# Negated row maxima of two heads turned by one group of F32R passes a unit

## The chip, the cores and the metric

One core of a Trainium2 chip. The metric is device time in microseconds (us): the median of the runs of the kernel before is 2976.83 us (three runs, 2974.4 to 2983.3).

## What is computed

One layer of a hybrid encoder over 2048 tokens of width 1024: a joint input projection; attention with 8 query heads over 2 key heads of width 64, beside a state space mixer (SSM); an output projection; a feed-forward network; a final norm. The change lies in the attention:

```
s = einsum('bqgrd,bkgd->bgrqk', q_blk, k) * scale
p = softmax(s, axis=-1)
o = einsum('bgrqk,bkgd->bqgrd', p, v)
```

The softmax subtracts each row's maximum before the exponential. Here the maximum is taken of scores that are computed once for that purpose, and its negative is added to the scores inside the matmul that makes them again, as one more operand row.

## The kernel before

The attention is cut into 16 units of 512 queries by two heads. For each unit, `prep_q` (line 685) loads and transposes the queries; `prep_max` (line 707) computes the scores of 32 blocks (4 groups of 512 keys, 2 heads, 4 blocks of 128 queries) with queries on the partitions (line 718), and VectorE (DVE) reduces each to its row maxima (line 719). `unit` (line 766) then computes the scores again with keys on the partitions: two passes a tile of 128 keys by 512 queries, `ka` with `qa` (line 790) and `kb` with `qb` (line 791), the exponential on ScalarE (ACT, line 793), and the product with the values (line 776). The sums of the exponentials are kept on DVE and GpSimd (POOL, lines 781 and 784).

The upper 64 partitions of `kb` hold ones (line 666), those of `qb` hold, for each query, the negative maximum in one row and zeros in the others. Their product adds the negative maximum to each score. The maxima come out of the reduction with queries on the partitions, and have to be turned to lie along a row. For this `mn`, two buffers for alternate units, has a block of 64 columns for each of the 8 (head, query block) pairs, all zero but for column 0, into which line 725 writes. Line 729 multiplies each block, as the stationary operand, with the fp32 identity: 4 fp32 matmuls of 128 columns a head, into the upper 64 partitions of one PSUM bank `ps_mt`. Line 730 copies them into `qb` of that head (ACT). The bank is the only one of the pool `ps_m` (tag "am"); the transposed queries (`ps_qt`, line 693), the sums and the transposed outputs (`ps_rs`, `ps_rt`, `ps_ot`, lines 742 to 755) take it in turn.

F32R is the 4-byte type that a matmul takes in a single pass; a plain fp32 matmul shows as two records in the trace. The scores run in F32R: `qa`, `qb`, `ka`, `kb` are written in it.

What sets the order: while `unit` goes through its 16 key tiles, it takes steps of the preparation of later units (`advance`, line 814, four yields a key tile, up to two units ahead) and of the SSM (`bg_ssm`, line 917), until its eight chunks are used up around unit 9. The program runs under a planner (`schedule_with_timeline_sim`, line 1497) that lays out each engine's queue at build time from simulated times; on the chip each engine goes through its queue in that order. After the attention the output projection (line 996) and the feed-forward products (lines 1241 and 1371) have their PE order pinned.

Of the kernel before, what the change touches and what calls it, by code (L numbers as in the profile page):

```python
# [9 lines left out]
F32 = mybir.dt.float32  # L10
F32R = mybir.dt.float32r
AF = mybir.ActivationFunctionType
# [5 lines left out]
P = 128  # L18
# [3 lines left out]
HD = 64  # L22
# [46 lines left out]
def tile_encoder(ctx: ExitStack, tc: tile.TileContext, I, O, stop=None, dbg=None):  # L69
    nc = tc.nc  # L70
    V = nc.vector
    A = nc.scalar
    GP = nc.gpsimd
    T = nc.tensor
# [6 lines left out]
    def const(shape, name, dt=F32):  # L81
        return cp.tile(shape, dt, tag=name, name=name)
# [4 lines left out]
    ident = const([P, P], "ident")  # L87
# [48 lines left out]
    MUL, ADD, SUB = ALU.mult, ALU.add, ALU.subtract  # L136
# [499 lines left out]
    MUL, ADD, SUB = ALU.mult, ALU.add, ALU.subtract  # L636
    with ExitStack() as p2:
# [8 lines left out]
        kp = p2.enter_context(tc.tile_pool(name="kp", bufs=1, reuse_waits="tile"))  # L646
# [5 lines left out]
        def scores(u, name):  # L652
            return (next(turn) if u else ps_1).tile([P, 512], F32, tag="s1", name=name)

        def misc(name, tag="am"):
            return (ps_m if tag == "am" else ps_c).tile([P, 512], F32, tag=tag, name=name)

        lo, hi = slice(0, HD), slice(HD, P)
        ka = [[pool.tile([P, 512], F32R, tag=f"ka{i}{g}", name=f"ka{i}{g}") for g in range(4)] for i, pool in enumerate((eq, kp))]
        mn = [kp.tile([P, 8, HD], F32, tag=f"mn{i}", name=f"mn{i}") for i in range(2)]  # L660
        kb = [[kp.tile([P, 512], F32R, tag=f"kb{i}{g}", name=f"kb{i}{g}") for g in range(4)] for i in range(NKV)]
        for t in mn:
            GP.memset(t, 0.0)
        for i in range(NKV):
            for g in range(4):
                GP.memset(kb[i][g][hi].bitcast(F32), 1.0)
# [1 line left out]
        def prep_k(g, first):  # L668

            pt = scores(0, "ps_kt")  # L670
            for j in range(4):
                T.transpose(pt[:, P * j:P * (j + 1)], k_sb[g][:, j].rearrange("q h e -> q (h e)"), ident)
            for half in (lo, hi):
                if first:
                    A.copy(ka[0][g][half], pt[lo])
                else:
                    A.copy(ka[1][g][half], pt[hi])
            if not first:
                for i, own in enumerate((lo, hi)):
                    V.tensor_sub(kb[i][g][lo], pt[own], ka[i][g][own])  # L680
# [26 lines left out]
        def prep_max(u):  # L707

            kv = (u % 4) // 2
            qa, qb = units[u]  # L710
            mx = eq.tile([P, 8, 4], F32, tag="mx", name="mx", bufs=2)
            for f in range(4):
                if u == 0 and f == 3:
                    prep_k(3, True)
                for h in range(2):
                    for j in range(4):
                        p1_ = scores(u, "ps_s1")
                        T.matmul(p1_, qa[h][:, P * j:P * (j + 1)], ka[kv][f], start=True, stop=True)  # L718
                        red = V.reduce_max(mx[:, 4 * h + j, f:f + 1], p1_, axis=AX.X)  # L719
                        yield  # L720
            maxima.append(red)
            m8 = aq.tile([P, 8], F32, tag="m8", name="m8")
            V.reduce_max(m8, mx, axis=AX.X)
            mt = mn[u % 2]
            V.tensor_scalar(mt[:, :, 0], m8, -1.0, None, op0=MUL)
            for h in range(2):
                pm = misc("ps_mt")
                for j in range(4):
                    T.matmul(pm[hi, P * j:P * (j + 1)], mt[:, 4 * h + j, :], ident, start=True, stop=True)
                A.copy(qb[h][hi], pm[hi])  # L730
                yield

        def finish(u, po, acc):
# [70 lines left out]
        def prep_all():  # L804
            for u in range(1, 16):
                for g in (prep_q(u), prep_max(u)):
                    for _ in g:
                        yield u
            yield 16
# [111 lines left out]
        with tc.high_priority(KOFF):  # L921
            for g in range(3):
                prep_k(g, True)
            for _ in chain(prep_q(0), prep_max(0)):
                pass
            for g in range(4):
                prep_k(g, False)
# [573 lines left out]
```

## Time and profile before

| | |
|---|---|
| median of three runs | 2976.83 us |
| the profiled execution: time, span | 2980.86 us, 2979.1 us |
| mean granted clock of TensorE, share of full speed | 0.961 |
| busy time of PE, PE weight loads, DVE, ACT, POOL | 2795.3, 2039.3, 1964.0, 1255.7, 1326.3 us |
| attention units (first to last start of a pass of line 790) | 379.9 to 1338.6 us |

Times in the trace count from the start of the span. PE is TensorE's matmul side, PEld its weight loads, which overlap it. A PE record's duration is its latency; back to back, records overlap, so the distance of two starts is what a pass costs in the queue. A line of a timeline merges records of one kind that follow each other: its second number reaches from the first start to the last end. "Idle before" is the time in which the engine waited, with what ended it.

### The profile page before, as it was taken

Reading aid. Unit: us, or ns where it says so; the run is one execution under the profiler, and the core shown is the slowest. Engines: PE = TensorE matmul, PEld = TensorE weight load, DVE = VectorE, ACT = ScalarE, POOL = GpSimd, SP = SyncE. Lnnn points to the kernel's source line nnn. Section 1 sums busy time; section 2 is a strip of 40 time slices with the busy share of each in tenths; the row PEclk is TensorE's granted clock in tenths of the full one; section 3 lists DMA queues with packets and bytes.
Section 4 is the critical chain, followed back from the end, with each engine's and each line's share of the span. In section 5 each row is a group of like instructions: output and inputs, shape, how many; then the busy total and the mean of one; then the engine's idle time right before and its main releaser. Section 6 shows DMA issues by size and latency. Waiting matters only on the chain. (4 is left out here: it accounts for less than half of the span.)

```text
span 2979.1 us, 37166 instructions
## 1 busy us (share of the span) xinstructions
PE 2795.3 (94%) x13020; PEld 2039.3 (68%) x13020; DVE 1964.0 (66%) x2815; ACT 1255.7 (42%) x2609; POOL 1326.3 (45%) x1122
## 2 busy tenths in 40 slices
PE   6998988978988899998998999999999999999998
PEld 4776844544444455546886788887878888888876
DVE  6879977677877755655666777777244677775243
ACT  3654554544444455553334434445222344443222
POOL 3648467868888887542334333331001333321000
PEclk8999999989998999998999999999999999999999
DMA  7764221111110010003447333338664333336573
GB/s 214 219 231 144 98 72 43 50 46 46 47 50 25 29 36 11 8 11 124 142 134 243 118 113 114 113 111 297 206 233 152 117 114 114 113 108 235 191 235 118
DMA packets 306506, 359.42 MB, mean 121 GB/s; under 512 B 50104, under 2 KB 222864, under 8 KB 305296
## 3 DMA queue, kind: packets, MB, share of 16 engines
q1 hardware_dynamic: 306320, 357.06, 36.8%
q8 instruction: 102, 1.67, 0.2%
q14 instruction: 84, 0.69, 0.1%
HBM read 249.53 MB, written 107.45 MB: 120 GB/s over the span
## 5 line engine op out<-in xcount | busy, mean ns | idle before, releaser
L1241 PE MATMUL ps_ha<-xc,w 128*128 128x512 f32 x2112 | 499.4, 392 | 14.3 <-ACT w L1201 8.4
L1371 PE MATMUL ps_f<-wo,act_i 128*128 128x512 f32 x2112 | 485.2, 392 | 6.8 <-DVE x2r L1389 4.3
L1241 PEld LDWEIGHTS ps_ha<-xc,w 128*128 128x128 f32 x2112 | 399.3, 189 | 99.9 <-ACT w L1201 8.8
L1371 PEld LDWEIGHTS ps_f<-wo,act_i 128*128 128x128 f32 x2112 | 399.3, 189 | 92.0 <-DVE x2r L1389 6.1
L719 DVE TENSOR_REDUCE mx<-ps_s 128x1 f32<-128x512 f32 x512 | 333.4, 682 | 110.5 <-PE ps_s L718 108.5
L1267 POOL TENSOR_TENSOR act_o<-th,act_o 128x512 fp32r<-128x512 f32 x88 | 115.2, 1309 | 486.4 <-ACT act_o L1266 473.0
L1202 DVE TENSOR_TENSOR wo<-wo_raw,wo 128x512 fp32r<-128x512 f32 x176 | 121.4, 702 | 295.3 <-ACT wo L1201 295.3
L1202 DVE TENSOR_TENSOR w<-w_raw,w 128x512 fp32r<-128x512 f32 x220 | 207.1, 959 | 117.3 <-ACT w L1201 117.3
L718 PE MATMUL ps_s<-ka,qa 128*128 128x512 f32 x512 | 212.2, 454 | 47.1 <-DVE mx L719 45.4
L1241 PE MATMUL ps_hb<-xc,w 128*128 128x512 f32 x1056 | 247.3, 389 | 0.0
L374 PE MATMUL ps_z<-whi,ht 128*128 128x512 f32 (+1 forms) x768 | 226.2, 379 | 16.0 <-ACT ht L363 12.1
L790 PE MATMUL ps_st<-qa,ka 128*128 128x512 f32 x512 | 224.8, 439 | 14.9 <-ACT e__6959 L793 2.5
L1201 ACT CAST wo<-wo_raw 128x512 fp32r<-128x512 f32 x176 | 107.7, 622 | 309.1 <-PE ps_f L1371 293.2
L1241 PEld LDWEIGHTS ps_hb<-xc,w 128*128 128x128 f32 x1056 | 198.1, 188 | 41.1
L718 PEld LDWEIGHTS ps_s<-ka,qa 128*128 128x128 f32 x512 | 94.0, 192 | 189.4 <-DVE mx L719 133.9
L791 PE MATMUL ps_st<-qb,kb 128*128 128x512 f32 x512 | 208.2, 407 | 0.1
L996 PE MATMUL ps_y<-wo,mt 128*128 128x512 f32 x768 | 189.1, 402 | 7.5 <-ACT mt L989 6.8
L996 PEld LDWEIGHTS ps_y<-wo,mt 128*128 128x128 f32 x768 | 146.1, 192 | 41.8 <-ACT mt L989 7.2
L374 PEld LDWEIGHTS ps_z<-whi,ht 128*128 128x128 f32 x768 | 141.1, 199 | 45.5 <-ACT ht L363 14.2
L790 PEld LDWEIGHTS ps_st<-qa,ka 128*128 128x128 f32 x512 | 99.0, 193 | 101.0 <-issue 22.5
L1395 POOL TENSOR_TENSOR sm<-ss 128x1 f32<-128x1 f32 x16 | 4.3, 268 | 367.4 <-ACT jk L1391 367.4
L134 POOL TENSOR_TENSOR w_sum<-w_raw 128x512 f32<-128x512 f32 x44 | 75.9, 1724 | 192.6 <-DVE wo L1202 96.6
(2279 smaller groups left out, 5721.8 us busy)
## 6 DMA issues: line engine op xcount, KB each, us to landing
w_raw<-in_w_ffn_in_dram SPq DMA_DIRECT2D x176, 256.0 KB
act_d<-act_o SPq DMA_DIRECT2D x88, 512.0 KB
wo_raw<-in_w_ffn_out_dram SPq DMA_DIRECT2D x176, 256.0 KB
act_i<-act_d SPq DMA_DIRECT2D x88, 512.0 KB
wa<-in_w_ada_dram SPq DMA_DIRECT2D x48, 512.0 KB
xt<-in_x_dram SPq DMA_DIRECT2D x30, 512.0 KB
xc<-xf_d SPq DMA_DIRECT2D x56, 256.0 KB
rot_d<-rot SPq DMA_DIRECT2D x16, 512.0 KB
```

Source lines behind the costliest of these rows:

```text
L134: eng.tensor_tensor(o, a, b, op=op)
L374: T.matmul(pp[:, 0:c1 - c0], ht[:, a, k], w[:, k, c0:c1], start=k == 0 and j == 0, stop=k == KD - 1 and j == 2)
L718: T.matmul(p1_, qa[h][:, P * j:P * (j + 1)], ka[kv][f], start=True, stop=True)
L719: red = V.reduce_max(mx[:, 4 * h + j, f:f + 1], p1_, axis=AX.X)
L790: T.matmul(st_, ka[kv][k // 4][:, ks], qa[h], start=True, stop=False)
L791: T.matmul(st_, kb[kv][k // 4][:, ks], qb[h], start=False, stop=True)
L996: pin(T.matmul(out, lhs[:, a, k], rhs[w][k][:, cs_], start=first and n == 0, stop=final and n == last))
L1201: A.copy(w[:, 0], src)
L1202: eng.tensor_sub(w[:, 1], src, w[:, 0])
L1241: pin(T.matmul(out, wv[:, l, kk], xc[i][kk][:, a], start=first and kk == 0 and n == 0, stop=kk == KH - 1 and n == 2, skip_group_check=True))
L1267: GP.tensor_sub(ao[:, 1], d[th], ao[:, 0])
L1371: pin(T.matmul(pf[j, c], act[f][:, a, js], wt[f, c][:, l], start=f == 0 and m == 0, stop=f == KF - 1 and m == 2))
```

## The change

`mn` becomes four blocks of 128 columns in F32R. For a query block the negative maxima of the two heads stand in columns 64 and 65, and one F32R matmul with an F32R copy of the identity turns both: they come out in rows 64 and 65 of one PSUM bank. Each head's copy into `qb` takes all upper 64 rows, multiplied with a column of the identity that is one in the head's own row and zero in the others. There are four matmuls a unit and one tenure of the bank; there were eight and two.

```diff
-        mn = [kp.tile([P, 8, HD], F32, tag=f"mn{i}", name=f"mn{i}") for i in range(2)]
+        mn = [kp.tile([P, 4, P], F32R, tag=f"mn{i}", name=f"mn{i}") for i in range(2)]
+        identr = kp.tile([P, P], F32R, tag="identr", name="identr")
+        A.copy(identr, ident)
         kb = [[kp.tile([P, 512], F32R, tag=f"kb{i}{g}", name=f"kb{i}{g}") for g in range(4)] for i in range(NKV)]
         for t in mn:
-            GP.memset(t, 0.0)
+            GP.memset(t.bitcast(F32), 0.0)
...
             mt = mn[u % 2]
-            V.tensor_scalar(mt[:, :, 0], m8, -1.0, None, op0=MUL)
+            V.tensor_scalar(mt[:, :, HD:HD + 2], m8.rearrange("q (h j) -> q j h", h=2), -1.0, None, op0=MUL)
+            pm = misc("ps_mt")
+            for j in range(4):
+                T.matmul(pm[:, P * j:P * (j + 1)], mt[:, j, :], identr, start=True, stop=True)
             for h in range(2):
-                pm = misc("ps_mt")
-                for j in range(4):
-                    T.matmul(pm[hi, P * j:P * (j + 1)], mt[:, 4 * h + j, :], ident, start=True, stop=True)
-                A.copy(qb[h][hi], pm[hi])
+
+                A.activation(qb[h][hi], pm[hi], AF.Copy, scale=ident[hi, HD + h:HD + h + 1])
                 yield
```

## Rows read from the trace of the kernel before

**Rows 1.** The page's table of engines: busy us, share of the span, instructions.

```profile
PE 2795.3 (94%) x13020; PEld 2039.3 (68%) x13020; DVE 1964.0 (66%) x2815; ACT 1255.7 (42%) x2609; POOL 1326.3 (45%) x1122
```

**Rows 2.** Busy time by stretch: stretch, length, then as the heading row says.

```profile
core 0: us, PE busy (x) PEld busy (x) DVE busy (x) ACT busy (x) POOL busy (x), PEclk, DMA share, GB/s
390.00:1056.00 666.00, 581.16 (x2423) 317.50 (x2422) 512.31 (x547) 298.97 (x526) 547.67 (x362) 0.91 0.15 44
1056.00:1300.00 244.00, 243.91 (x1042) 126.37 (x1040) 144.53 (x232) 126.80 (x223) 161.36 (x131) 1.00 0.04 11
```

**Rows 3.** Waits, 390 to 1056 us: us in total, times, longest.

```profile
DVE mx L719 <- PE ps_s L718: 60.5, 64, 2.4
PE ps_s L718 <- DVE mx L719: 43.7, 22, 7.5
```

**Rows 4.** Groups by line, 390 to 1056 and 1056 to 1300 us: busy, mean ns, idle.

```profile
L729 PE MATMUL ps_mt<-ident,mn 128*64 128x128 f32 x145 | 24.0, 318 | 12.3 <-DVE mn L725 10.1 <-ACT qb L730 2.0
...
L729 PE MATMUL ps_mt<-ident,mn 128*64 128x128 f32 x96 | 12.5, 274 | 0.0
```

**Rows 5.** PE timeline, 1100 to 1112 us: start, first start to last end, what.

```profile
1101.59 0.59 PE L776 MATMUL ps_o<-e__9932,v_sb 128*64 128x512 f32 x1
1102.11 0.50 PE L790 MATMUL ps_st<-qa,ka 128*128 128x512 f32 x1
...
1103.72 0.59 PE L776 MATMUL ps_o<-e__9946,v_sb 128*64 128x512 f32 x1
1104.14 1.04 PE L729 MATMUL ps_mt<-ident,mn 128*64 128x128 f32 x8
1105.11 0.50 PE L790 MATMUL ps_st<-qa,ka 128*128 128x512 f32 x1
...
1110.25 0.66 PE L693 MATMUL ps_qt<-ident,qt 128*128 128x128 f32 x4
1110.66 0.48 PE L790 MATMUL ps_st<-qa,ka 128*128 128x512 f32 x1
```

**Rows 6.** PE timeline, 355 to 366 us: F32R passes of 256 columns.

```profile
357.64 0.28 PE L374 MATMUL ps_z<-wlo,ht 128*128 128x256 f32 x1
357.75 0.39 PE L374 MATMUL ps_z<-whi,ht 128*128 128x512 f32 x1
```

**Rows 7.** PE timeline, 460 to 463 us, in a stretch at the lower clock.

```profile
461.18 1.12 PE L693 MATMUL ps_qt<-ident,qt 128*128 128x128 f32 x4
461.95 0.78 PE L791 MATMUL ps_st<-qb,kb 128*128 128x512 f32 x1
```

**Rows 8.** PE timeline, 933 to 939 us, with the idle time before.

```profile
938.16 1.12 PE L693 MATMUL ps_qt<-ident,qt 128*128 128x128 f32 x4 [0.67 <-ACT qb L730]
```

**Rows 9.** PE timeline, 384 to 391 us, unit 0.

```profile
385.67 1.09 PE L729 MATMUL ps_mt<-ident,mn 128*64 128x128 f32 x8
...
389.01 1.09 PE L729 MATMUL ps_mt<-ident,mn 128*64 128x128 f32 x8
390.03 0.50 PE L791 MATMUL ps_st<-qb,kb 128*128 128x512 f32 x1
```

**Rows 10.** Groups by line on ACT, up to 400 us: busy, mean ns, idle.

```profile
L346 ACT ACTIVATE xt<-xt,rxb 128x1024 f32<-128x1024 f32 x16 | 18.4, 1151 | 8.2 <-POOL rxb L114 8.0
...
L872 ACT COPY r<-r 128x1024 f32<-128x1024 f32 x1 | 1.0, 1044 | 1.2 <-DMA q_d<-qo 1.2
```

**Rows 11.** Busy time by stretch, two stretches of 60 us, columns as in rows 2.

```profile
570.00:630.00 60.00, 44.79 (x185) 23.75 (x181) 47.37 (x47) 21.54 (x38) 42.98 (x30) 0.83 0.15 43
630.00:690.00 60.00, 51.15 (x215) 27.53 (x216) 43.25 (x44) 29.83 (x52) 51.23 (x35) 0.91 0.10 28
```

**Rows 12.** DVE timeline: the write of the maxima in four of the units.

```profile
650.93 0.60 DVE L725 TENSOR_SCALAR mn<-m 128x8 f32<-128x8 f32 x1
724.06 0.36 DVE L725 TENSOR_SCALAR mn<-m 128x8 f32<-128x8 f32 x1
795.41 1.04 DVE L725 TENSOR_SCALAR mn<-m 128x8 f32<-128x8 f32 x1
862.60 0.33 DVE L725 TENSOR_SCALAR mn<-m 128x8 f32<-128x8 f32 x1
```

## Prediction

> **What bounds the kernel now.** I began with the table of engines on the page: TensorE (PE) is busy for 94% of the span, far more than any other engine [rows 1]. That is an average, so the next view was the busy time by stretch, for the attention phase that the change touches [rows 2]. It falls into two parts. From 390 to 1056 us the units 1 to 9 run with the SSM chunks in between: PE is busy for 581 of 666 us at a granted clock of 0.91, VectorE (DVE) for 512. From 1056 to 1300 us the units 10 to 15 run almost alone: PE is busy for 243.9 of 244.0 us at a clock of 1.00, DVE for 145. So in the second part PE alone sets the pace, and each us taken from its queue is a us of the end. In the first part neither engine is full, and the waits tell who is late [rows 3]: the DVE reductions wait 60.5 us for score passes of PE, and PE waits 43.7 us for reductions to free a bank. They hand the lateness to and fro. After the attention PE runs the feed-forward products in a pinned order, so I take an earlier end of the attention to be carried to the end.
>
> The groups by line give the size of what is changed [rows 4]. The transposed maxima (line 729) hold PE for 24.0 us in the first part and 12.5 us in the second, 96 records there for six units: 16 a unit, two records for each fp32 matmul.
>
> **The change, part by part.** *Passes on PE, late units.* The PE timeline of unit 11 has the whole site [rows 5]. One head's group starts at 1104.14, 0.42 us after the last start of the value products, and the next instruction starts at 1105.11, 0.97 us later. There are two such sites in a unit: 2 x (0.42 + 0.97) = 2.78 us. One site vanishes; there the value products hand over straight to scores, which took 0.52 us (1101.59 to 1102.11). At the other, four F32R passes of 128 columns with 128-column weights stand. No row shows that form. Nearest is the query transpose, four records of the same shape: 1110.25 to 1110.66, 0.41 us. The entry costs 0.52, since the new passes fill the full array as scores do. New: 0.52 + 0.52 + 0.41 = 1.45 us. Saved: 2.78 - 1.45 = 1.33 us a unit, 8.0 us for six.
>
> Bounds of that pass: the F32R passes of 256 columns start 0.11 us apart [rows 6], so if columns alone counted, four of 128 would take 0.23 us; if F32R is no cheaper than fp32 at this width, the group costs 0.97 us as now. I take 0.41, the row of the same shape. The low end would give 16 x 0.18 = 2.9 us more, the high end take back 16 x 0.56 = 9.0 us. The Trainium skill ("TensorE: Matmul & The Clock Gate", Back-to-back issue gap) gives about 56 ns for an isolated pass of 128 columns; by it the group would be an estimated 0.22 us, at the low end, and it says itself that this leaves out the weight loads. No row here shows so short a spacing for full-width weights.
>
> *Passes on PE, units 1 to 9.* Out go the 24.0 us and the 2.0 us in which the second group waited for the first head's copy to free the one bank [rows 4]. In come nine groups: six at 0.41, and for three units where the clock stands at its lower level (1.2 GHz) 0.77 each, as the query transposes took there (461.18 to 461.95) [rows 7]: 4.8 us. The handovers cost 0.10 us a unit as above, 0.9. The one bank is now held until both copies are done, so a query transpose that follows at once waits for one copy more: in unit 8 it waited 0.67 us for one [rows 8]; 0.7 us in three units, 2.1. Left: 26.0 - 4.8 - 0.9 - 2.1 = 18.2 us. What of it reaches the end lies between nothing (PE then only waits longer for DVE, which is late next) and all. I take the share by who is late: 60.5 / (60.5 + 43.7) = 0.58 [rows 3], which gives 10.6 us.
>
> *Unit 0.* The second group (389.01) stands straight before the first scores with the maxima (390.03) [rows 9]: 1.0 us. The first one is followed by other preparation and is counted at nothing; at most 0.5 us more.
>
> *Copies on ScalarE (ACT).* The 32 copies become activations with a scale per row. Of 128x1024 elements, one with such a scale takes 1151 ns and a plain copy 1044 [rows 10], so 0.11 us more each, 3.4 us in all. I cost it at nothing: ACT is busy for 299 of 666 and 127 of 244 us [rows 2]. If that cover is gone it is 3.4 us at most. The first head's copy now waits for four passes that serve both heads, but those are shorter than its own eight records were. Behind it on ACT stand the exponentials, which PE's next scores wait for.
>
> *The rest.* The copy of the identity (once, a 128x128 tile) has to be there for the first group of unit 0 and lies among ACT's other work of the prologue; uncovered it is below the 1.04 us of a copy eight times its size [rows 10]. The write of the maxima is the same eight values on DVE, the memsets have the same bytes, no DMA is added, and the two yields per unit stay, so the interleaving counted in yields is the same.
>
> **Sum.** 8.0 + 10.6 + 1.0 = 19.6 us less. The profiled execution took 2980.9 us (span 2979.1); it would be 2961.3. It lies 4.0 us above the median of the three runs, so for the median: 2976.8 - 19.6 = 2957. What a measurement can tell from no change is 0.3%, 8.9 us.
>
> **The rivals.** *A. DVE keeps the first part.* Nothing of the 18.2 us arrives; only the late units and unit 0 gain: 9.0 us, 2968. For it: PE's longest waits there are for reductions, up to 7.5 us [rows 3]. Against: DVE waits for PE more than PE for DVE.
>
> *B. The emptied time cools PE.* In two neighbouring stretches PE was busy for 51.2 and 44.8 of 60 us, and the clock stood at 0.91 and 0.83 [rows 11], 0.0125 for each us. If all 18.2 us turn into waiting, that is 1.6 us in 60, a clock lower by 0.02, and 581 us of PE work longer by 2.2%, 12.8 us: 2968 + 12.8 = 2981. The same page of the Trainium skill (HAM oscillation) says this too, that PE left waiting is set back to its half rate. Against: in the first part slow passes mostly stand where PE was waiting anyhow, and in the second the clock is at 1.00 with no gap.
>
> *C. F32R at 128 columns is no cheaper than fp32*, so the change does only half of what it says. Late units 8.0 - 6 x 0.56 = 4.6; units 1 to 9 (18.2 - 5.0) x 0.58 = 7.7; unit 0 1.0: 13.3 us, 2963.
>
> *D. The order is laid anew, and worse.* The planner that orders the instructions at build works with simulated times (line 1497); shorter passes and one bank tenure less shift the order of units 1 to 9 on every engine. Those units do alike work, yet one took 73.1 us (650.93 to 724.06) and another 67.2 (795.41 to 862.60) [rows 12]. If the new order costs half that spread, 2.95 us, in each of nine units and the saving there is lost: +26.6 - 9.0 = 17.6 us, 2994. It turns the sign once it costs over 1.0 us a unit. For it: this part lives on who is late to whom. Against: a new order can as well be better, and PE has less to place.
>
> **How the numbers follow.** Forecast 0.50, A 0.17, B 0.10, C 0.08, D 0.15. Everything arriving with the cheapest pass is 8.0 + 20.3 (no bank wait) + 1.5 + 2.9, about 33: 2944, the low end. The upper end takes in A, B and the nearer part of D: 2984. Faster by over 0.3% (under 2967.9): the forecast, C, and A, which lies on the line, in a third of its cases: 0.64. Within: the rest of A and B: 0.21. Slower: D: 0.15.
>
> **What would show it.** Line 729 with four records a unit, about 0.1 us apart and without the second bank wait; units 10 to 15 shorter by 1.3 us each; DVE's waits for scores down by some 10 us in units 1 to 9 and the clock there still near 0.91. It is wrong if the start-to-start of the late units does not move, if the records stay 0.2 us apart, or if units 1 to 9 together change by more than 20 us either way, which would be the order.

## The result and the profile after

The changed kernel takes 2944.3 us, median of six runs (2939.3 to 2948.0), against 2976.9 us for the kernel before beside it. The ratio is 0.9888, with a 95% interval of 0.9876 to 0.9900: 33 us faster, where 20 were forecast. The profiled execution took 2948.0 us, with a span of 2945.9. The passes, line 729 before, are line 730 now, their copies into `qb` line 733 (730 before); other lines between 719 and 882 stand two or three further down.

The page's table of engines, kernel after (compare [rows 1]):

```profile
PE 2766.8 (94%) x12828; PEld 2014.8 (68%) x12828; DVE 1973.1 (67%) x2815; ACT 1258.6 (43%) x2610; POOL 1338.2 (45%) x1122
```

There are 192 PE records fewer, as 16 units with 16 records have become 16 with 4. Busy time by stretch, kernel after (engines in the order of [rows 2]):

```profile
390.00:1056.00 666.00, 590.73 (x2423) 315.99 (x2424) 536.68 (x571) 315.71 (x554) 583.50 (x381) 0.93 0.15 45
1056.00:1300.00 244.00, 243.76 (x1002) 119.34 (x1000) 142.72 (x230) 132.03 (x231) 157.18 (x129) 1.00 0.04 11
```

In the first stretch DVE is busy for 537 us instead of 512, PE for 591 instead of 581, although the change gives DVE no work and takes some from PE. More other work lies in the same 666 us. The last passes of the scores (line 793 after, 790 before) start at 1300.7 us, where it was 1338.6. Groups by line, kernel after, first in 390 to 1056 us and then in 1056 to 1300 us (compare [rows 4]):

```profile
L733 ACT ACTIVATE qb<-ps_mt,ident 64x512 fp32r<-64x512 f32 x20 | 12.6, 676 | 10.5 <-PE ps_mt L730 10.5
L730 PE MATMUL ps_mt<-identr,mn 128*128 128x128 f32 x40 | 7.1, 303 | 4.1 <-DVE mn L727 4.1
...
L730 PE MATMUL ps_mt<-identr,mn 128*128 128x128 f32 x20 | 2.9, 267 | 0.0
```

The passes hold PE for 7.1 and 2.9 us where it was 24.0 and 12.5, and the 2.0 us wait for the first head's copy is gone. The stretches now hold the groups of ten and five units, where it was nine (and one record) and six. Waits, kernel after, 390 to 1056 us (compare [rows 3]):

```profile
DVE mx L721 <- PE ps_s L720: 65.3, 67, 2.3
PE ps_s L720 <- DVE mx L721: 44.1, 25, 4.4
ACT r L875 <- DVE xs L885: 22.4, 6, 7.8
DVE qa L699 <- ACT qa L698: 15.8, 5, 5.7
ACT qb L733 <- PE ps_mt L730: 10.5, 7, 4.9
```

The last three, in the kernel before:

```profile
ACT r L872 <- DVE xs L882: 41.9, 7, 13.9
DVE qa L697 <- ACT qa L696: 37.0, 8, 9.6
ACT qb L730 <- PE ps_mt L729: 31.4, 18, 5.2
```

DVE and PE wait for each other as much as before; the forecast had DVE's waits for scores down by some 10 us. What shrank by some 20 us each are waits on ACT or for it, and only the last of the three names the changed work. So the question was how much of the 33 us belongs to the passes and how much to the order that the planner laid anew.

### The profile page after: what moved, and what is told of

Read it like the earlier page. It is cut to its first block, busy times and chain, and to the rows that moved or that the text cites. A ratio compares the mean times of both kernels' runs of the same rounds, so it can differ in the third digit from the quotient of the medians.

```text
span 2945.9 us, 36806 instructions
## 1 busy us (share of the span) xinstructions
PE 2766.8 (94%) x12828; PEld 2014.8 (68%) x12828; DVE 1973.1 (67%) x2815; ACT 1258.6 (43%) x2610; POOL 1338.2 (45%) x1122
```

## Experiments

All ratios are against the kernel before, run on the same chip beside each.

| run | us | ratio, 95% interval |
|---|---|---|
| new_in_old_order | 2957.0 | 0.9925 [0.9911, 0.9940] |
| old_in_new_order | 2975.3 | 0.9988 [0.9974, 1.0001] |
| fp32_in_new_order | 2947.8 | 0.9903 [0.9887, 0.9920] |
| fp32_in_old_order | 2962.3 | 0.9953 [0.9938, 0.9969] |
| eight_f32r | 2963.6 | 0.9949 [0.9935, 0.9964] |
| eight_f32r_old_order | 2968.5 | 0.9965 [0.9953, 0.9978] |
| old_order_copy_later | 2981.7 | 1.0005 [0.9996, 1.0015] |
| new_order_copy_later | 2946.0 | 0.9893 [0.9877, 0.9909] |
| copy_in_program_order | 2944.5 | 0.9885 [0.9869, 0.9901] |
| fp32_planned | 2949.3 | 0.9902 [0.9887, 0.9917] |
| f32r_in_fp32_order | 2945.2 | 0.9888 [0.9873, 0.9903] |
| before_slower_ssm | 2986.2 | 1.0029 [1.0017, 1.0040] |
| before_copy_kept | 2966.2 | 0.9954 [0.9938, 0.9971] |
| before_copy_kept_slower | 2959.4 | 0.9932 [0.9918, 0.9947] |
| after_copy_kept_slower | 2937.6 | 0.9859 [0.9844, 0.9873] |

### The passes and the order, one at a time

To part the two, each engine's queue (PE, DVE, ACT, POOL, SP) was held in an order given as a list of instruction numbers: an edge ties each instruction to the one before it on its engine, without a semaphore. No run holds a kernel in its own order unchanged, but new_order_copy_later below holds the changed kernel in its own order but for seven copies and is level with it (0.9893 against 0.9888), so holding costs nothing that shows.

```diff
+def hold_order(tc, packed):
+    nums = np.cumsum(np.frombuffer(zlib.decompress(base64.b85decode(packed)), np.int16).astype(np.int64))
+    by = {i.name: i for i in tc.nc.cur_bb.bb.instructions}
+    last = {}
+    for n in nums:
+        i = by[f"I-{n}"]
+        if i.engine in last:
+            tc.add_manual_dep(i, last[i.engine], mybir.DependencyInfo(mybir.DependencyClass.NoSync, mybir.DependencyReason.DATA))
+        last[i.engine] = i.name
...
         tile_encoder(tc, aps, out)
+        hold_order(tc, ORDER)
```

**new_in_old_order**: the changed instructions in the order of before; the four passes stand where the first head's four matmuls stood.

> The changed kernel's instructions, with every engine's queue held in the order of the kernel before: the four F32R passes stand where the first head's group stood, the second head's group is gone, the copies stay at their places. Theory 'passes' (PE time alone made the 33 us, the order nothing): 2944 us. Theory 'both' (the passes give the 20 us of the forecast, the planner's new order the rest): 2957. Theory 'order alone': 2977.

**old_in_new_order**: the instructions of before in the order of after; all eight matmuls stand where the four passes stand.

> The kernel before, with every engine's queue held in the order of the changed kernel: both heads' groups of fp32 passes stand, one behind the other, where the four F32R passes stand there, the second waiting for the first copy (0.67 us a unit more on PE at worst, 11 us in all). 'Passes': no gain, 2977 to 2988. 'Both': 13 us of gain less up to 6 for that wait, 2964 to 2970. 'Order alone': 2944 to 2950.

**fp32_in_new_order** and **fp32_in_old_order**: the changed kernel with its four passes in plain fp32, in either order.

```diff
-        mn = [kp.tile([P, 4, P], F32R, tag=f"mn{i}", name=f"mn{i}") for i in range(2)]
-        identr = kp.tile([P, P], F32R, tag="identr", name="identr")
+        mn = [kp.tile([P, 4, P], F32, tag=f"mn{i}", name=f"mn{i}") for i in range(2)]
+        identr = kp.tile([P, P], F32, tag="identr", name="identr")
```

> The changed kernel with its four passes in fp32 instead of F32R, every engine's queue held in the order of the changed kernel. The group costs 0.97 instead of 0.4 us on PE, 16 x 0.56 = 9.0 us in all. 'Passes': all of it arrives, 2953. 'Both', with the forecast's shares (all in six late units, 0.58 in nine): 3.4 + 2.9 = 6.3, 2951. 'Order alone': 2944.

> The changed kernel with its four passes in fp32, in the order of the kernel before. In the new order fp32 cost 4 us more than F32R. If PE's time reaches the end in full (9.0 us by the forecast's sizes): 2966. If as in the new order: 2961. If the type is nothing and the half number of passes and one tenure are all: 2957.

In the old order the change is worth 0.75%, 22 us; the new order adds 0.37% (0.9925 to 0.9888), 11 us. The trace shows where. The write of the maxima to `mn` marks the units; the DVE timeline of before has it at 385.3 us in unit 0, 1056.35 in unit 10 and 1286.43 in unit 15. The same lines of the DVE timeline, new_in_old_order:

```profile
381.62 0.17 DVE L727 TENSOR_SCALAR mn<-m 128x8 fp32r<-128x8 f32 x1
...
1036.31 0.96 DVE L727 TENSOR_SCALAR mn<-m 128x8 fp32r<-128x8 f32 x1
...
1260.59 0.16 DVE L727 TENSOR_SCALAR mn<-m 128x8 fp32r<-128x8 f32 x1
```

and of the kernel after:

```profile
383.59 0.17 DVE L727 TENSOR_SCALAR mn<-m 128x8 fp32r<-128x8 f32 x1
...
1023.11 0.30 DVE L727 TENSOR_SCALAR mn<-m 128x8 fp32r<-128x8 f32 x1
...
1248.58 0.21 DVE L727 TENSOR_SCALAR mn<-m 128x8 fp32r<-128x8 f32 x1
```

From unit 0 to 10 it is 671.0 us before, 654.7 with the passes alone and 639.5 after; from 10 to 15 it is 230.1, 224.3 and 225.5. So the passes give 16.3 us in the units beside the SSM and 5.8 in five late units; the new order gives 15.2 beside the SSM and takes 1.2 late. These are single executions, and the one of before was 4.0 us above its median.

Where the order's gain lies shows in PE's busy time between the marks of units 0 and 10 (window, length, PE busy and records, clock, DMA share, GB/s). Before, new_in_old_order and after:

```profile
385.34:1056.35 671.01, 584.48 (x2447) 0.91 0.15 46
381.62:1036.31 654.69, 562.32 (x2327) 0.91 0.16 47
383.59:1023.11 639.52, 562.98 (x2304) 0.93 0.15 44
```

With the passes alone PE is busy for 22.2 us less and idle for 92.4 us instead of 86.5. The new order leaves the busy time as it is and brings the idle time down to 76.5: the order's gain is time in which PE stood still. The waits of PE that shrank most, 390 to 1056 us, are those for reductions (44.1 us after, shown above) and for the write of the maxima. Two lines of new_in_old_order, then one of after:

```profile
PE ps_s L720 <- DVE mx L721: 50.4, 23, 6.7
PE ps_mt L730 <- DVE mn L727: 10.3, 5, 5.3
PE ps_mt L730 <- DVE mn L727: 4.1, 3, 3.0
```

Of the three waits on ACT in the section before, new_in_old_order has 41.1, 32.8 and 12.9 us, and old_in_new_order 25.8, 33.1 and 28.7: the first goes with the order, the last with the instructions, the second only with both.

The new order with the old instructions is also faster beside the SSM (382.1 to 1040.09, 658.0 us), but slower late (1040.09 to 1278.15, 238.1 us), which leaves 3.6 us by its ratio, hardly told from none, and less than theory 'both' had. Most of the late loss lies between units 10 and 11 (52.6 us, before 45.8), where this order still has products of the last SSM chunk, 44 records of lines 901 and 902 in PE's queue. In the three units behind it the loss is 1.3 to 1.5 us each, and 0.67 of that is one wait. PE timeline of unit 11, old_in_new_order:

```profile
1093.90 0.40 PE L791 MATMUL ps_st<-qb,kb 128*128 128x512 f32 x1
1094.23 1.09 PE L729 MATMUL ps_mt<-ident,mn 128*64 128x128 f32 x8
1095.99 1.09 PE L729 MATMUL ps_mt<-ident,mn 128*64 128x128 f32 x8 [0.67 <-ACT qb L730]
1097.01 0.50 PE L790 MATMUL ps_st<-qa,ka 128*128 128x512 f32 x1
```

With the two groups side by side the second one waits 0.67 us until the first head's copy has freed the single bank. One group with one tenure doesn't have this wait, and needs no gap between two groups in the queue.

The type shows in PE's queue as well. PE timeline of unit 11, fp32_in_old_order:

```profile
1089.32 1.16 PE L730 MATMUL ps_mt<-identr,mn 128*128 128x128 f32 x8
1090.24 0.48 PE L793 MATMUL ps_st<-qa,ka 128*128 128x512 f32 x1
```

Four full-width fp32 passes take 0.92 us there, in two records each; in F32R it is 0.49 (1084.25 to 1084.74, shown further down).

In fp32 the four passes lose 0.28% (8 us) in the old order and 0.15% (4.5 us, the intervals overlap) in the new one. Merging two groups into one, still in fp32, is worth 0.47% in the old order (14 us).

### Eight passes in F32R

**eight_f32r** is the kernel before with eight full-width F32R passes in two groups, planned anew. It has one `mn` buffer where before has two, for space; what that costs was not tried by itself.

```diff
-        mn = [kp.tile([P, 8, HD], F32, tag=f"mn{i}", name=f"mn{i}") for i in range(2)]
+        mn = [kp.tile([P, 8, P], F32R, tag="mn0", name="mn0")]
+        identr = kp.tile([P, P], F32R, tag="identr", name="identr")
+        A.copy(identr, ident)
...
-                    T.matmul(pm[hi, P * j:P * (j + 1)], mt[:, 4 * h + j, :], ident, start=True, stop=True)
+                    T.matmul(pm[:, P * j:P * (j + 1)], mt[:, 4 * h + j, :], identr, start=True, stop=True)
```

> The kernel before with eight F32R passes of full width instead of eight fp32 ones, two tenures of the bank and plain copies (one buffer of the maxima's blocks instead of two, for space); the planner orders it anew. PE saves 2 x 0.56 = 1.1 us a unit. 'Passes': 18 us and the low clock units, about 2957. 'Both' and 'order alone': the planner's order decides as much as the passes, anywhere from 2945 to 2980.

**eight_f32r_old_order** is the same, held in the order of before.

> Eight full-width F32R passes a unit in two tenures of the bank (2963.6 us when planned anew), held in the order of the kernel before. If that plan's new order is worth nothing, this is the same, 2960 to 2967, and the type alone is worth 11 to 17 us with two tenures. If the new order of that plan carried a gain like the changed kernel's (13 us), this is 2973 to 2979, and the type alone is worth next to nothing. If that plan's order was a loss, it is under 2960.

The type, with the one buffer, is worth 0.35% in the old order, 10 us, between the two ranges expected, and merging on top of it 0.40% (0.9965 to 0.9925), 12 us. Taken the other way round it was 14 us for the merging and 8 for the type, so both are about of one size. Planning this version anew adds 0.16%, within what the two intervals leave open: this new plan carries little, and much less than the changed kernel's.

### One copy of the SSM

ACT's longest waits in the old order were for one instruction, the copy `r<-r` of the decay rows, once a chunk, which stands behind scans of the chunk before. ACT timeline of new_in_old_order:

```profile
604.01 1.04 ACT L875 COPY r<-r 128x1024 f32<-128x1024 f32 x1 [13.30 <-DVE xs L885]
```

In the kernel after the same kind of wait is 22.4 us in all instead of 41.1. The theory was that ACT stands still there with exponentials behind it. Three runs tried it. **old_order_copy_later** is new_in_old_order with seven of the eight copies four or five places later in ACT's list; **new_order_copy_later** moves them up to four places later in the order of after; **copy_in_program_order** is the changed kernel, planned freely but for this:

```diff
-            A.copy(r0, r8[:, gs].unsqueeze(2).to_broadcast([P, GC, M]))
+            tc.keep_in_program_order(A.copy(r0, r8[:, gs].unsqueeze(2).to_broadcast([P, GC, M])))
```

> The changed kernel's instructions in the order of the kernel before, with one thing of that order mended: ACT's copies of the SSM decay factors (line 875), which wait for VectorE's scans of the chunk before (41.1 us in all, one of 13.3), stand four to five ACT instructions later in ACT's queue (no more is possible without a deadlock), so that exponentials run meanwhile. Theory 'that copy' (the new order gains because these waits are shorter, 22.4 us): it recovers most of the 13 us between this order (2957.0) and the new one, 2944 to 2949. Theory 'many handovers': 2953 to 2957.

> The changed kernel in its own order, with the same copies up to four ACT instructions later. 'That copy': a further gain of up to half of the 22.4 us, 2933 to 2940. 'Many handovers': 2942 to 2945.

> The changed kernel with one edit: the copy of the decay factors may not be laid ahead of what stands before it in the program; the planner lays out the rest anew. 'That copy': no long wait for the scans, 2933 to 2942, unless the rest of the new order is worse. 'Many handovers': like any other order, 2944 to 2960.

The first one is 25 us slower than with the copies in their old places. The wait has moved, as the waits from 390 to 1056 us of old_order_copy_later show:

```profile
POOL r L876 <- ACT r L875: 31.9, 6, 12.5
```

ACT no longer waits, but POOL's writes into `r`, and the scans that need them, wait for the copy. The other two stand level with the changed kernel. The theory falls: that wait is a place where lateness shows, not its cause.

### Does the order come with the structure?

**fp32_planned** is the changed kernel with the fp32 edit shown above, planned anew; **f32r_in_fp32_order** is the changed kernel, held in the order that this plan has.

> The changed kernel with its four passes a unit in plain fp32 (mn and the identity in fp32), planned anew and free. In the order of the changed kernel these fp32 passes took 2947.8 us, in the order of the kernel before 2962.3. Theory S (the new order's gain comes with the structure: one group and one tenure of the bank a unit): this plan has the gain as well, 2944 to 2952. Rival P (the planner found the better order because F32R passes are short in its simulated time): without the short passes the gain is gone, 2958 to 2966. Rival R (an order's worth is as good as random, since the queues meet by chance): neither, 2952 to 2958 or over 2966.

> The instructions of the changed kernel (four F32R passes), every engine's queue held in the order that the planner lays for the fp32 version of the same four passes. S: 2941 to 2948, as the changed kernel. P: 2953 to 2960, as the changed instructions in the order of before (2957.0). R: anything else. In all three it stands 4 to 8 us below the fp32 run beside it, which is what the type was worth in the two orders tried.

Both came out as theory S said. All three free plans of the one-group structure (the changed kernel, copy_in_program_order and fp32_planned) have the gain, so it isn't the short F32R passes in the planner's times that bring it. Whether it needs the one group is tried next.

### How much attention lies beside the SSM

What the orders with the gain share is a count: how many exponentials have started when the last scan of the SSM does. Windows from 385 us to the start of the last scan, exponentials alone (window, length, ACT busy and count, then clock, DMA share, GB/s). The kernel before:

```profile
385.00:997.60 612.60, 165.52 (x284) 0.90 0.15 45
```

new_in_old_order:

```profile
385.00:978.40 593.40, 165.28 (x284) 0.92 0.15 44
```

the kernel after:

```profile
385.00:1000.30 615.30, 178.90 (x307) 0.93 0.15 45
```

A unit has 32 exponentials. With the same instructions, the order of after puts 23 more beside the SSM, and the SSM ends 21.9 us later: 30 us for a unit's worth, while in new_in_old_order the 229 remaining took 334 us, 47 a unit (last one at 1312.5 us). The difference is 23/32 x (47 - 30) = 12 us, about the new order's gain. That is bookkeeping, not yet a cause: an order that is faster for another reason would show it too. Of the kernels so far, all runs in the order of before and eight_f32r have 284 (one of them a table load), the runs in the order of after 307, and the other plans of the one-group structure 303 to 322. old_order_copy_later has 284 as well and is 25 us slower than new_in_old_order. The last four runs spread the SSM by other means, three of them in the kernel before.

**before_slower_ssm**, the kernel before with a lower rate of SSM steps, planned anew:

```diff
-BGR = 15
+BGR = 12
```

**before_copy_kept** has the edit of copy_in_program_order instead; **before_copy_kept_slower** has both; **after_copy_kept_slower** is the changed kernel with both.

> The kernel before (eight fp32 matmuls, two tenures) with the SSM taken at 12 steps in 16 key tiles where it was 15, planned anew. Its last chunk's copy of the decay rows stands behind 254 exponentials in ACT's queue, behind 244 in the kernel before and 257 in the changed one. Theory W (what the new order changes is the mix: the same eight SSM chunks lie beside more attention, so that DVE's load is thinner while they last): 10 of the 13 exponentials of that spread, so some 10 of the 13 us, 2964 to 2971. Rival S2 (the gain of the new order needs the single tenure of the bank): no gain, 2973 to 2981.

> The kernel before with the chunks' copies kept in program order on ACT, planned anew. The last one stands behind 276 exponentials (244 in the kernel before; 284 in the changed kernel with the same edit, which took 2944.5). W: the whole gain of the spread or more, 2958 to 2966, with the instructions of before. S2: 2973 to 2981.

> The run beside it with 12 SSM steps in 16 key tiles as well: the last copy behind 344 exponentials, so the SSM reaches unit 11. W: no worse than the run beside it as long as PE has room beside the SSM, 2952 to 2966; if thinner is better without end, under 2958. S2: 2973 to 2981. If the SSM's passes now only lie on PE's full stretch, it gives the gain back: over 2970.

> The changed kernel with both edits: copies kept in program order and 12 SSM steps in 16 key tiles, the last copy behind 344 exponentials. The changed kernel with the first edit alone took 2944.5. W: at or below the changed kernel, 2932 to 2946, and if below 2936 it is the version that beats both. S2: the spread is no lever, 2944 give or take 4 as any plan of the single tenure. Given back on PE's full stretch: over 2950.

The same windows to the last scan, before_slower_ssm:

```profile
385.00:1021.80 636.80, 173.89 (x296) 0.93 0.15 43
```

before_copy_kept:

```profile
385.00:1023.60 638.60, 180.80 (x310) 0.92 0.14 43
```

before_copy_kept_slower:

```profile
385.00:1071.40 686.40, 205.11 (x351) 0.95 0.14 41
```

after_copy_kept_slower:

```profile
385.00:1063.00 678.00, 208.28 (x356) 0.94 0.14 41
```

Against the kernel before, before_copy_kept has 26 more exponentials for 26.0 us and before_copy_kept_slower 67 more for 73.8: 32 and 35 us a unit (unit 0 begins up to 3 us apart in these runs, which is worth up to 4 us a unit), and both are faster, by 0.46% and 0.68%, without the change. after_copy_kept_slower is the fastest of all, by 0.26 to 0.29% against the changed kernel with or without the kept copies, about what a measurement can tell. That speaks for W and against S2: the single tenure isn't needed for such a gain. But before_slower_ssm, with 12 more exponentials for 24.2 us (65 a unit), is slower by 0.29%, where W said 10 us faster. Its waits from 390 to 1056 us:

```profile
DVE mx L719 <- PE ps_s L718: 71.4, 66, 4.7
...
PE ps_mt L729 <- DVE mn L725: 16.5, 4, 6.3
```

They are 11 and 6 us longer than before ([rows 3]; [rows 4] has the 10.1 us). PE also waits 8.5 us instead of 1.9 for the reciprocals of the sums (line 755 for line 751). So the count alone doesn't decide; how the queues meet does as well. W holds at best as a lever, not as a law: two plans of the kernel before gained, one lost, and that plans differ by chance of how the queues meet is not excluded by so few. Why this plan has those waits was not settled.

The four runs leave another reading of the change itself: between plans of the same kind it is worth 0.75% in the order of before, 0.69% with the copies kept (0.9954 to 0.9885) and 0.73% with the copies kept and the slower SSM (0.9932 to 0.9859): 22, 21 and 22 us. In the order of after, where two groups fit badly, the same exchange is worth 1.00% (0.9988 to 0.9888), 30 us.

## Why the prediction was right and wrong

Two steps failed: the order, held at nothing, gained 11 us, and of units 0 to 9 the sum had too little PE time going. That the measured 2944.3 stands at the low end of the range, 2944, is luck: that end was made of the cheapest passes with everything arriving, and neither came about.

**The bound** was read rightly but for unit 10. In the units behind it PE alone sets the pace: they move with its queue. And the earlier end of the attention carries to the end: the last scores start 37.9 us earlier, and 33.2 of that arrive at the end of the span. The stretch behind the last scores took 1637 to 1646 us in the profiled executions, after at 1645 and before at 1640, so the rest is within that spread.

**Late units**: forecast 1.33 us a unit, measured (230.1 - 224.3) / 5 = 1.16 from unit 10 to 15. The write of the maxima in units 11 and 14, before and then new_in_old_order (DVE timeline):

```profile
1102.15 0.18 DVE L725 TENSOR_SCALAR mn<-m 128x8 f32<-128x8 f32 x1
1238.98 0.20 DVE L725 TENSOR_SCALAR mn<-m 128x8 f32<-128x8 f32 x1
1082.16 0.17 DVE L727 TENSOR_SCALAR mn<-m 128x8 fp32r<-128x8 f32 x1
1215.10 0.20 DVE L727 TENSOR_SCALAR mn<-m 128x8 fp32r<-128x8 f32 x1
```

From 11 to 14 it is (136.83 - 132.94) / 3 = 1.30 a unit, nearly the forecast. From 10 to 11 nothing was gained (45.80, then 45.85 us). There PE came to wait for a reduction, which it did not before; waits of PE, 1036 to 1082 us, new_in_old_order:

```profile
PE ps_s L720 <- DVE mx L721: 1.2, 1, 1.2
```

Of the terms the group was mis-sized by a little. PE timeline of unit 11, new_in_old_order:

```profile
1083.72 0.59 PE L779 MATMUL ps_o<-e__9883,v_sb 128*64 128x512 f32 x1
1084.25 0.66 PE L730 MATMUL ps_mt<-identr,mn 128*128 128x128 f32 x4
1084.74 0.45 PE L793 MATMUL ps_st<-qa,ka 128*128 128x512 f32 x1
```

The entry took 0.53 (forecast 0.52) and the four passes 0.49, not 0.41. In the order of after the group stands behind a score pass. PE timeline of unit 11, kernel after:

```profile
1074.11 0.39 PE L794 MATMUL ps_st<-qb,kb 128*128 128x512 f32 x1
1074.34 0.56 PE L730 MATMUL ps_mt<-identr,mn 128*128 128x128 f32 x4
1074.73 0.45 PE L793 MATMUL ps_st<-qa,ka 128*128 128x512 f32 x1
```

There it is 0.39. So the row of the same shape was the right one to take, and the low end of the bound (0.23) and the high end (0.97) were both far off.

**Units 0 to 9**: 18.2 us removed and a share of 0.58 gave 10.6, with 1.0 for unit 0. Measured 16.3, which with the forecast's 18.2 would be a share of (16.3 - 1.0) / 18.2 = 0.84. But PE's busy time between the marks fell by 22.2 us, and 5.8 came back as idle time, where the forecast's share left 7.6 to waiting. So the step that failed is the time removed, more than the share: PE and DVE do hand part of it back, about a quarter here, not 42%. 17.9 of the 22.2 us are the passes themselves (25.9 us of line 729 before, 8.0 of line 730 in new_in_old_order); where the other 4.3 come from stays open. Two terms of the 18.2 were off as well. The query transposes' longer wait for the bank was put at 2.1 us, and new_in_old_order has 1.3 us of it, against 0.7 before. And the handovers, put at 0.10 us a unit, are 0.20 by the forecast's own sum for the late units (twice 0.52 for twice 0.42).

**The copies on ACT**, costed at nothing: 676 ns instead of 580 to 583, +0.10 us where +0.11 was forecast, and ACT's wait for `ps_mt` fell from 31.4 to 10.5 us. That nothing of it came through wasn't tried by itself.

**The sum**, with order and instructions parted: 19.6 forecast, 21 to 22 measured in three pairs of plans. The interval of new_in_old_order reaches from 18 to 27 us, so as a whole this part of the sum isn't told from the forecast.

**The order** is the step that failed outright. The prediction said of it that a new order can as well be better, but the sum held it at nothing and only rival D gave it a price, as a loss of 26.6 us. It gained 11, by less idle time of PE beside the SSM (76.5 us for 92.4). The sign that the prediction gave for it came up: units 0 to 9 together changed by 31.5 us (671.0 to 639.5), over the 20 that "would be the order". How much an order can move was to be seen in the rows: units of the same work that took 73 and 67 us [rows 12]. It called for a term of either sign, and for a low end of the range some 10 us lower than the cheapest passes made it.

**The rivals.** A falls: 16.3 us arrive in the first part. B falls: the clock between the marks of units 0 and 10 is 0.91 with the passes alone, as before, and 0.93 after. C falls as a condition, as F32R is cheaper, but its size was right: four fp32 passes in the old order give 14 us, and C said 13.3. D is right that the order moves the time, here by half as much as the instructions, and wrong in its sign; old_order_copy_later and before_slower_ssm show that a plan can lose 8 to 25 us as well.

## What to carry to other kernels

Where a planner lays every queue anew, a change has two effects, its own and that of the new order; holding the order of before under the new instructions parts them (22 and 11 us here). A forecast should give the order a term of either sign, sized by how far alike units differ in the trace. And before taking a gain as the change's, try other plans of both kernels: the difference between like plans (21 to 22 us in three pairs) was steadier than either plan's own time, as long as the order fits both: in the order of after it was 30 us.

## What was not expected of the hardware

A 128-column F32R pass with 128-column weights takes 0.10 us of PE's queue behind score passes (0.39 us for four) and 0.12 behind the value products (0.49). The 56 ns of an isolated pass that the prediction quoted don't show. The Trainium skill ("TensorE: Matmul & The Clock Gate", LDWEIGHTS (loading the stationary operand)) prices a weight load by its columns at 1.2 a nanosecond, an estimated 107 ns for 128. The spacing of 0.10 to 0.12 us lies near that, while the records of these loads are 0.19 us long from 1056 to 1300 us of after.

Attention placed beside the SSM cost 30 to 35 us a unit where it cost 47 alone, except in one plan (65). In the changed kernel this is less idle time of PE; no single wait was found that accounts for all of it.
